# Sums of squares of q and k in fp32, a softplus series with one instruction a step, and four row casts on ScalarE, in a hybrid attention and DeltaNet block

## The chip, the cores and the metric

The kernel runs on one core of one Trainium2 chip. The metric is device time in microseconds (us) of one execution. Engines are named as in the profile: PE (TensorE matmul), PEld (its weight loads), DVE (VectorE), ACT (ScalarE), POOL (GpSimd) and SP (SyncE, which here only issues DMAs). Each engine works through its own queue strictly in the order written, and waits on semaphores for the others.

## The reference, cut to what matters

One layer of a streaming encoder: 16 meta tokens and 512 tokens of width 1024 go through RMSNorm, then through two parallel branches (forgetting attention, and a gated delta rule over chunks of 64), then a ConvFFN. The change touches the front end of the gated delta rule and nothing else:

```python
def l2_norm(x):
    return x * lax.rsqrt(jnp.sum(x * x, axis=-1, keepdims=True) + RMS_EPS)

gdn_qkv = jax.nn.silu(causal_dwconv(gdn_qkv, gdn_conv_w))       # q, k, v: 8 heads of 64
log_f = jax.nn.log_sigmoid(fox_f + fgt_bias)
beta  = jax.nn.sigmoid(gdn_b)
g     = -jnp.exp(gdn_a_log) * jax.nn.softplus(gdn_a + gdn_dt_bias)
q = l2_norm(q) * (dk ** -0.5);  k = l2_norm(k)
gc = jnp.cumsum(g, axis=-1)                                      # within each chunk
decay = jnp.exp(jnp.where(tril, gc[..., :, None] - gc[..., None, :], NEG_INF))
lmat = jnp.where(strict, jnp.einsum('bhncd,bhnsd->bhncs', kb, k) * decay, 0.0)
```

So there are sums of squares over the 64 channels of each head, for q and for k, at all 528 tokens. All three small gates come from a softplus of 3 x 8 values per token. From the logarithms of these sums and from `gc` the kernel makes rows of 8 heads by 576 padded tokens, whose differences are the exponents of `decay`.

## The kernel before, in words

**Products.** Activations lie with channels on the 128 partitions and the 528 tokens along the free axis. A weight tile of 128 output channels is loaded as fp32 and split in two: `hi` is a rounded fp32r copy, made on ACT (L131), and `lo = raw - hi`, made on DVE, or on POOL for the input tiles 5 to 8 (L132, `POOL_LO`). `product` then issues three fp32r matmuls for each 128 x 128 block (L139 to L141): hi by hi, hi by lo, lo by hi. An input projection is 48 such matmuls, in two halves of 264 tokens.

**Order.** The input projections run in a written order (`PLAN` and the list `order`): first the small gates (tile 0), then k (tiles 1 to 4), q (5 to 8), v (9 to 12), then output gates and attention projections, which fill PE while the delta rule goes on. The framework's scheduler turns the program into one queue per engine. It uses its own estimate of when each operand is ready, so an edit in one place can move instructions far behind it in all queues.

**The part that changes.** `gdn_tile(kind, pair, ss)` handles one tile of two heads, eight times: four of k (`kind` 0) and then four of q (`kind` 1). DVE scales the projection into `y` (L626). ACT starts a four-tap causal convolution in `cv` (L631), DVE adds three taps (L633), ACT takes a tanh (L636), and DVE multiplies into `kq` (L641, L642). Then come the squares. ACT squares `kq` twice, once into the fp32r tile `sqh` and once into the fp32 tile `sq` (L647, L648). POOL makes `sql = sq - sqh` (L649), and PE sums both over the 64 channels of each head, with a 128 x 8 matrix of zeros and ones (`selR`, fp32r) as the stationary operand, into two PSUM banks (L653, L654). `sqh` and `sql` live in single buffers (tags LS and X). After four tiles ACT takes the logarithms of the sums (L684 to L686). The logarithm and the tanh need different ACT tables, so an ACT_TABLE_LOAD stands wherever the one follows the other.

**Softplus.** The gate projection is transposed to 120 columns on 128 partitions. The logarithm is a series in s2 on DVE: a multiply (L578) and an add (L579) for each of seven coefficients, then L580 and L581. Its result `sp` is transposed back on PE (`ps_m` L591, `ps_r` L593) and scaled on DVE (L594 to L596). Three groups use one `ps_m` tile, so each group's transpose waits for the DVE reads of the group before.

**Rows.** L692 to L702 make the 8 x 576 rows. Four of these instructions are plain casts to fp32r on DVE (L698 twice, L700, L701). Their results go to POOL, which builds the operands of the chunk products (L725, L728), on which PE's `ps_d` and `ps_e` (L735, L739) rest.

**Later.** Nine chunks are prepared and scanned, attention runs in four pairs of heads (scores `ps_s`, values `ps_fo`, the transposed v `ps_fv`), and the rest is branch products (`bg`, `bf`), the output projection and the ConvFFN.

Of the kernel before, what the change touches and what calls it, by code (L numbers as in the profile page):

```python
# [12 lines left out]
F32 = mybir.dt.float32  # L13
F32R = mybir.dt.float32r
I32 = mybir.dt.int32
AF = mybir.ActivationFunctionType
ALU = mybir.AluOpType
# [4 lines left out]
P = 128  # L22
D = 1024
KT = D // P
T = 528
NM = 16
# [7 lines left out]
TP = NCH * C  # L34
EPS = 1e-6
GATES = list(range(8, 16)) + list(range(8))
TMPB = {'y': 2, 'cv': 2, 'th': 1, 'sq': 1}
SZB = 2
SOLVEP = 300
BF_A = 3  # L40
# [3 lines left out]
INORDER = ()  # L44
W0K = 2
CC_AT = 1
SS_DVE = ()
N_WARM = 8
LAG = 0
X_AHEAD = 1  # L50
# [31 lines left out]
C_HM, C_PM, C_SG, C_SEL, C_M0, C_M1, C_HM2, C_R1, C_R2, C_AB = 0, 2, 6, 7, 39, 151, 279, 281, 409, 473  # L82
# [4 lines left out]
def hybrid_block(ctx: ExitStack, tc: tile.TileContext, xT, w_in, w_bg, w_bf, w_out, w_up, w_down,  # L87
                 par, consts, out, dbg=None):
    nc = tc.nc
    act, dve, pool, pe = nc.scalar, nc.vector, nc.gpsimd, nc.tensor  # L90
# [13 lines left out]
    cst = keep.tile([P, C_N], F32, name="cst")  # L104
# [131 lines left out]
    with tc.tile_pool(name="inp", bufs=1) as inp:  # L236
# [19 lines left out]
        for k in range(KT):  # L256
# [14 lines left out]
            sq = acc if k in (0, SQ_POOL[0]) else inp.tile([P, T], F32, tag="sq", bufs=3, name="sq")  # L271
# [223 lines left out]
    with ExitStack() as gctx:  # L495
        gp = gctx.enter_context(tc.tile_pool(name="gp", bufs=1))

        subp = proj_ctx.enter_context(tc.tile_pool(name="sp", bufs=1, side="right"))

        ep_ctx = ExitStack()  # L500
        ep = ep_ctx.enter_context(tc.tile_pool(name="ep", bufs=1, side="right"))
# [4 lines left out]
        def main(ap):  # L506
            return ap.rearrange("p (n c) -> p n c", c=C)
# [3 lines left out]
        pool.memset(hmE.bitcast(F32), 0.0)  # L511
        dve.tensor_copy(hmE[0:40].rearrange("p (a b) -> p a b", b=C),
                        cst[0:40, C_HM:C_HM + 2].unsqueeze(2).broadcast_to([40, 2, C]))
        selR = ep.tile([P, 32], F32R, name="selR")
        pool.tensor_copy(selR, cst[:, C_SEL:C_SEL + 32])
        nA = gp.tile([8, 1], F32, name="nA")
        act.activation(nA, prm[0:8, PG_AL:PG_AL + 1], AF.Exp)
        dve.tensor_scalar(nA, nA, -1.0, None, op0=ALU.mult)
# [5 lines left out]
        R1, R2, KB, AB = [], [], [], ep.tile([104, 2, TP], F32R, name="AB")  # L524
# [48 lines left out]
        dve.reciprocal(s2, s2)  # L573
        dve.tensor_tensor(se, se, s2, op=ALU.mult)
        dve.tensor_tensor(s2, se, se, op=ALU.mult)
        dve.tensor_scalar(sr, s2, 1.0 / 17, 1.0 / 15, op0=ALU.mult, op1=ALU.add)
        for m in (13, 11, 9, 7, 5, 3, 1):
            dve.tensor_tensor(sr, sr, s2, op=ALU.mult)  # L578
            dve.tensor_scalar(sr, sr, 1.0 / m, None, op0=ALU.add)  # L579
        dve.scalar_tensor_tensor(sr, se, 2.0, sr, op0=ALU.mult, op1=ALU.mult)  # L580
        dve.scalar_tensor_tensor(sp.rearrange("p a b -> p (a b)"), sxf, 0.0, sr, op0=ALU.max, op1=ALU.add)  # L581


# [22 lines left out]
        for j in range(5):  # L606
            w = min(P, T - j * P)
# [11 lines left out]
        CUT = NM + 256  # L619

        def gdn_tile(kind, pair, ss=None):
# [19 lines left out]
            dve.scalar_tensor_tensor(d0, th[:, 0:NM], 1.0, a[:, 0:NM], op0=ALU.add, op1=ALU.mult)  # L641
            dve.scalar_tensor_tensor(d1, main(th[:, NM:]), 1.0, main(a[:, NM:]), op0=ALU.add, op1=ALU.mult)  # L642
            sq = tmp("sq", f"sq{idx}")

            sqh, sql = (subp.tile([P, 1024], F32R, tag=t, name=n)[:, 0:T] for t, n in (("LS", f"sqh{idx}"), ("X", f"sql{idx}")))
            for t in (sqh, sq):
                act.activation(t[:, 0:NM], d0, AF.Square)  # L647
                act.activation(main(t[:, NM:T]), d1, AF.Square)  # L648
            (dve if kind * 4 + pair in SS_DVE else pool).tensor_tensor(sql, sq, sqh.bitcast(F32), op=ALU.subtract)  # L649
            sel = selR[:, pair * 8:pair * 8 + 8]  # L650
            for i, t in enumerate((sqh, sql)):
                first, last = pair == 0 and i == 0, pair == 3 and i == 1
                pe.matmul(ss[0][0:8, 0:CUT], sel, t[:, 0:CUT], start=first, stop=last)  # L653
                pe.matmul(ss[1][0:8, 0:256], sel, t[:, CUT:], start=first, stop=last)  # L654

        def v_tile(p):

# [37 lines left out]
        dve.scalar_tensor_tensor(br, lnk, -0.5, gc, op0=ALU.mult, op1=ALU.subtract)  # L695
        dve.tensor_tensor(main(kl), main(br), main(gc)[:, :, C - 1:C].broadcast_to([8, NCH, C]), op=ALU.add)
        for w in range(2):
            dve.tensor_copy(AB[0:8, w], ar[w])  # L698
            dve.tensor_tensor(AB[32:40, w], ar[w], AB[0:8, w].bitcast(F32), op=ALU.subtract)
        dve.tensor_copy(bh, br)  # L700
        dve.tensor_copy(AB[64:72, 0], bh.bitcast(F32))  # L701
        dve.tensor_tensor(AB[96:104, 0], br, bh.bitcast(F32), op=ALU.subtract)  # L702

        tokf = gp.tile([C, NCH, 2, 8], F32, name="tokf")
# [659 lines left out]
```

## Time and profile before

| what | value |
|---|---|
| three timed runs | 877.65, 878.01, 878.02 us (median 878.01) |
| the profiled execution | 877.7 us; its span is 875.8 us, so 1.9 us lie outside the span |
| PE busy | 839.6 us of the span (96%) |
| DVE, ACT, POOL busy | 585.5 us (67%), 392.6 us (45%), 140.5 us (16%) |
| PE clock granted | full nearly everywhere, mean 0.991 |

The page's digits by slice say that PE is at 9 tenths or more nearly everywhere, with dips in the first three slices, and DVE is at 9 tenths in most of the first six. The table of stages and the timeline by engine say more than the page does, because the change lies between 36 and 110 us. In a timeline row the first number is the start in us from the beginning of the span and the second is the duration in us. Then come engine, line, operation, tiles and shape. A bracket at the end holds the idle time before the instruction and what released it. Rows of matmuls overlap, since a matmul's duration runs from its issue to its last write: what one costs PE is the distance between two starts.

### The profile page before, as it was taken

Reading aid. Unit: us, or ns where it says so; the run is one execution under the profiler, and the core shown is the slowest. Engines: PE = TensorE matmul, PEld = TensorE weight load, DVE = VectorE, ACT = ScalarE, POOL = GpSimd, SP = SyncE. Lnnn points to the kernel's source line nnn. Section 1 sums busy time; section 2 is a strip of 40 time slices with the busy share of each in tenths; the row PEclk is TensorE's granted clock in tenths of the full one; section 3 lists DMA queues with packets and bytes.
Section 4 is the critical chain, followed back from the end, with each engine's and each line's share of the span. In section 5 each row is a group of like instructions: output and inputs, shape, how many; then the busy total and the mean of one; then the engine's idle time right before and its main releaser. Section 6 shows DMA issues by size and latency. Waiting matters only on the chain. (4 is left out here: it accounts for less than half of the span.)

```text
span 875.8 us, 17084 instructions
## 1 busy us (share of the span) xinstructions
PE 839.6 (96%) x7088; PEld 801.0 (91%) x7088; DVE 585.5 (67%) x1066; ACT 392.6 (45%) x611; POOL 140.5 (16%) x167
## 2 busy tenths in 40 slices
PE   7978999999999999899999999999999999999995
PEld 7977999999999999788999999999999999888884
DVE  7999998697266678787654676677766677232324
ACT  6655554523433485855354454434444344332321
POOL 4353575100000201100522100000000000010113
PEclk9999999999999999989999999999999999999997
DMA  7312233627432341335623223333223332333322
GB/s 229 107 49 73 74 97 99 149 93 176 127 116 74 92 140 61 98 103 150 218 98 97 89 83 95 97 97 95 80 92 98 97 96 77 99 91 107 91 67 96
DMA packets 52240, 91.27 MB, mean 104 GB/s; under 512 B 24438, under 2 KB 27646, under 8 KB 52164
## 3 DMA queue, kind: packets, MB, share of 16 engines
q1 hardware_dynamic: 51060, 89.14, 33.9%
q8 instruction: 55, 0.90, 0.5%
q10 hardware_dynamic: 1104, 1.05, 0.4%
q14 instruction: 21, 0.17, 0.1%
HBM read 80.01 MB, written 10.16 MB: 103 GB/s over the span
## 5 line engine op out<-in xcount | busy, mean ns | idle before, releaser
L140 PE MATMUL ps_in<-xl,hi_in 128*128 128x264 f32 (+2 forms) x720 | 197.8, 285 | 2.5 <-DVE xl L264 2.5
L139 PE MATMUL ps_in<-xh,hi_in 128*128 128x264 f32 (+2 forms) x720 | 197.4, 287 | 1.7 <-ACT hi_in L131 1.2
L140 PE MATMUL ps_up<-ul,hi_up 128*128 128x256 f32 (+1 forms) x704 | 198.7, 282 | 0.0
L141 PE MATMUL ps_in<-xh,lo_in 128*128 128x264 f32 (+2 forms) x720 | 196.7, 286 | 1.9 <-DVE lo_in L132 1.9
L141 PE MATMUL ps_up<-uh,lo_up 128*128 128x256 f32 (+1 forms) x704 | 198.4, 282 | 0.0
L139 PE MATMUL ps_up<-uh,hi_up 128*128 128x256 f32 (+1 forms) x704 | 198.0, 282 | 0.0
L140 PEld LDWEIGHTS ps_in<-xl,hi_in 128*128 128x128 f32 x720 | 132.8, 188 | 4.0 <-DVE xl L264 3.1
L139 PEld LDWEIGHTS ps_in<-xh,hi_in 128*128 128x128 f32 x720 | 132.0, 188 | 4.5 <-ACT hi_in L131 1.9
L141 PEld LDWEIGHTS ps_in<-xh,lo_in 128*128 128x128 f32 x720 | 132.0, 188 | 3.8 <-DVE lo_in L132 2.6
L139 PEld LDWEIGHTS ps_up<-uh,hi_up 128*128 128x128 f32 x704 | 133.0, 189 | 0.0
L141 PEld LDWEIGHTS ps_up<-uh,lo_up 128*128 128x128 f32 x704 | 132.8, 189 | 0.0
L140 PEld LDWEIGHTS ps_up<-ul,hi_up 128*128 128x128 f32 x704 | 132.7, 188 | 0.0
L1197 DVE TENSOR_TENSOR u<-ps_up,rstd 128x258 f32<-128x258 f32 x88 | 37.2, 425 | 56.6 <-PE ps_up L141 56.6
L139 PE MATMUL ps_dn<-fh,hi_dn 128*128 128x512 f32 (+1 forms) x198 | 73.5, 371 | 0.0
L140 PE MATMUL ps_dn<-fl,hi_dn 128*128 128x512 f32 (+1 forms) x198 | 73.0, 369 | 0.0
L141 PE MATMUL ps_dn<-fh,lo_dn 128*128 128x512 f32 (+1 forms) x198 | 73.0, 369 | 0.0
L132 DVE TENSOR_TENSOR lo_dn<-raw_dn,hi_dn 128x1024 fp32r<-128x1024 f32 (+1 forms) x25 | 29.0, 1160 | 61.2 <-ACT hi_dn L131 61.2
L131 ACT ACTIVATE hi_in<-raw_in 128x1024 fp32r<-128x1024 f32 x43 | 45.0, 1054 | 51.3 <-PE ps_in L140 33.4
L1232 POOL TENSOR_TENSOR acc<-acc,sq 128x512 f32<-128x512 f32 (+1 forms) x7 | 11.2, 1607 | 353.1 <-ACT sq L1230 353.1
L131 ACT ACTIVATE hi_up<-raw_up 128x1024 fp32r<-128x1024 f32 x44 | 46.7, 1061 | 37.8 <-PE ps_up L140 28.3
L132 DVE TENSOR_TENSOR lo_up<-raw_up,hi_up 128x1024 fp32r<-128x1024 f32 x44 | 53.9, 1225 | 14.3 <-ACT hi_up L131 14.3
L131 ACT ACTIVATE hi_dn<-raw_dn 128x1024 fp32r<-128x1024 f32 (+1 forms) x25 | 24.8, 993 | 74.9 <-PE ps_dn L140 70.0
(339 smaller groups left out, 1655.8 us busy)
## 6 DMA issues: line engine op xcount, KB each, us to landing
raw_up<-w_up SPq DMA_DIRECT2D x44, 512.0 KB, 3.5
raw_in<-w_in SPq DMA_DIRECT2D x43, 512.0 KB, 4.0
raw_dn<-w_down SPq DMA_DIRECT2D x17, 512.0 KB, 3.5
gd<-g SPq DMA_DIRECT2D x16, 257.0 KB, 4.2
gt<-gd SPq DMA_DIRECT2D x16, 257.0 KB, 2.7
raw_o<-w_out SPq DMA_DIRECT2D x8, 512.0 KB, 3.5
raw_dn<-w_down SPq DMA_DIRECT2D x8, 384.0 KB, 3.1
xr<-xT SPq DMA_DIRECT2D x8, 264.0 KB, 4.4
```

What stands on the lines that cost most here:

```text
L131: act.activation(hi[:, a:a + step], raw[:, a:a + step], AF.Copy)
L132: (eng or dve).tensor_tensor(lo[:, a:a + step], raw[:, a:a + step], hi[:, a:a + step].bitcast(F32), op=ALU.subtract)
L139: pe.matmul(ps, wh[:, ws], xh[:, k0 + i, a:b], start=first and i == 0, stop=False)
L140: pe.matmul(ps, wh[:, ws], xl[:, k0 + i, a:b], start=False, stop=False)
L141: pe.matmul(ps, wl[:, ws], xh[:, k0 + i, a:b], start=False, stop=last and i == k - 1)
L1197: dve.tensor_tensor(y[:, a:b], ps[:, :b - a], rstd2[:, a:b], op=ALU.mult)
L1232: pool.tensor_tensor(acc[:, a:b], acc[:, a:b], sq, op=ALU.add)
```

## The change

Three edits, in one function of the program:

- `gdn_tile` squares once, into an fp32 tile `sq` with two buffers (`TMPB`). `sqh`, `sql`, the POOL subtraction and `selR` are gone. The sums are one matmul per PSUM bank and tile, with fp32 operands on both sides, in place of two in fp32r.
- The softplus series is arranged so that each of its seven steps is one instruction, (sr + 1/m) * s2. One extra instruction doubles `se`, and the last product adds the leading 1.
- The four casts of the rows are activations on ACT; the second of the casts of `br` reads the fp32 row itself instead of the rounded one.

```diff
-TMPB = {'y': 2, 'cv': 2, 'th': 1, 'sq': 1}
+TMPB = {'y': 2, 'cv': 2, 'th': 1, 'sq': 2}
...
-        selR = ep.tile([P, 32], F32R, name="selR")
-        pool.tensor_copy(selR, cst[:, C_SEL:C_SEL + 32])
...
-        dve.tensor_scalar(sr, s2, 1.0 / 17, 1.0 / 15, op0=ALU.mult, op1=ALU.add)
-        for m in (13, 11, 9, 7, 5, 3, 1):
-            dve.tensor_tensor(sr, sr, s2, op=ALU.mult)
-            dve.tensor_scalar(sr, sr, 1.0 / m, None, op0=ALU.add)
-        dve.scalar_tensor_tensor(sr, se, 2.0, sr, op0=ALU.mult, op1=ALU.mult)
+        dve.tensor_scalar(sr, s2, 1.0 / 17, None, op0=ALU.mult)
+        for m in (15, 13, 11, 9, 7, 5, 3):
+            dve.scalar_tensor_tensor(sr, sr, 1.0 / m, s2, op0=ALU.add, op1=ALU.mult)
+        dve.tensor_scalar(s2, se, 2.0, None, op0=ALU.mult)
+        dve.scalar_tensor_tensor(sr, sr, 1.0, s2, op0=ALU.add, op1=ALU.mult)
...
             sq = tmp("sq", f"sq{idx}")
-
-            sqh, sql = (subp.tile([P, 1024], F32R, tag=t, name=n)[:, 0:T] for t, n in (("LS", f"sqh{idx}"), ("X", f"sql{idx}")))
-            for t in (sqh, sq):
-                act.activation(t[:, 0:NM], d0, AF.Square)
-                act.activation(main(t[:, NM:T]), d1, AF.Square)
-            (dve if kind * 4 + pair in SS_DVE else pool).tensor_tensor(sql, sq, sqh.bitcast(F32), op=ALU.subtract)
-            sel = selR[:, pair * 8:pair * 8 + 8]
-            for i, t in enumerate((sqh, sql)):
-                first, last = pair == 0 and i == 0, pair == 3 and i == 1
-                pe.matmul(ss[0][0:8, 0:CUT], sel, t[:, 0:CUT], start=first, stop=last)
-                pe.matmul(ss[1][0:8, 0:256], sel, t[:, CUT:], start=first, stop=last)
+            act.activation(sq[:, 0:NM], d0, AF.Square)
+            act.activation(main(sq[:, NM:T]), d1, AF.Square)
+            sel = cst[:, C_SEL + pair * 8:C_SEL + pair * 8 + 8]
+            pe.matmul(ss[0][0:8, 0:CUT], sel, sq[:, 0:CUT], start=pair == 0, stop=pair == 3)
+            pe.matmul(ss[1][0:8, 0:256], sel, sq[:, CUT:], start=pair == 0, stop=pair == 3)
...
-            dve.tensor_copy(AB[0:8, w], ar[w])
+            act.activation(AB[0:8, w], ar[w], AF.Copy)
             dve.tensor_tensor(AB[32:40, w], ar[w], AB[0:8, w].bitcast(F32), op=ALU.subtract)
-        dve.tensor_copy(bh, br)
-        dve.tensor_copy(AB[64:72, 0], bh.bitcast(F32))
+        act.activation(bh, br, AF.Copy)
+        act.activation(AB[64:72, 0], br, AF.Copy)
```

The change is nine lines shorter, so the line numbers of its later part are 9 lower (the logarithms at L684 to L686 become L675 to L677). The scheduler gives every queue a new order from the first projections up to the branch products `bf`; behind these, PE's order is that of the kernel before. Three places matter below.

**DVE, around the third tile of k.** `cv2` and `cv3` are the convolutions of tiles 2 and 3 of k, `y3` and `y4` evacuate projections, `kq` takes the product with the tanh, and `ogT` rows are softplus steps. Before:

```order
L578 TENSOR_TENSOR ogT_108<-ogT_108 128x120
L626 TENSOR_TENSOR y3_619<-ps_in4_627,rstdh_115 128x264
L633 SCALAR_TENSOR_TENSOR cv2_598<-y2_539,prm_73,cv2_598 128x527
L579 TENSOR_SCALAR ogT_108<-ogT_108 128x120
L633 SCALAR_TENSOR_TENSOR cv2_598<-y2_539,prm_73,cv2_598 128x526
L578 TENSOR_TENSOR ogT_108<-ogT_108 128x120
L633 SCALAR_TENSOR_TENSOR cv2_598<-y2_539,prm_73,cv2_598 128x525
```

The change:

```order
L572 TENSOR_TENSOR ogT_108<-ogT_108 128x120
L630 SCALAR_TENSOR_TENSOR cv2_576<-y2_517,prm_73,cv2_576 128x527
L573 TENSOR_SCALAR ogT_108<-ogT_108 128x120
L623 TENSOR_TENSOR y3_590<-ps_in4_598,rstdh_115 128x264
L630 SCALAR_TENSOR_TENSOR cv2_576<-y2_517,prm_73,cv2_576 128x526
L575 SCALAR_TENSOR_TENSOR ogT_108<-ogT_108 128x120
L630 SCALAR_TENSOR_TENSOR cv2_576<-y2_517,prm_73,cv2_576 128x525
```

The first tap of tile 2 has moved ahead of the evacuation of `y3`, and the softplus begins its steps later in the queue, with one instruction for each.

**ACT, at the logarithms of k's sums.** `ps_ss` are the sums, `th` the tanhs, `sq` and `sqh` the squares. Before:

```order
L684 ACT_TABLE_LOAD
L684 ACTIVATE LA_442<-ps_ss_489,epsb_76 8x64
L685 ACTIVATE LA_442<-ps_ss_489,epsb_76 8x256
L686 ACTIVATE LA_442<-ps_ss_490,epsb_76 8x256
L636 ACT_TABLE_LOAD
L636 ACTIVATE th5_848<-cv5_843 128x528
```

The change:

```order
L675 ACT_TABLE_LOAD
L675 ACTIVATE LA_434<-ps_ss_481,epsb_76 8x64
L676 ACTIVATE LA_434<-ps_ss_481,epsb_76 8x256
L633 ACT_TABLE_LOAD
L633 ACTIVATE th4_732<-cv4_727 128x528
L677 ACT_TABLE_LOAD
L677 ACTIVATE LA_434<-ps_ss_482,epsb_76 8x256
L641 ACTIVATE sq4_736<-kq_478 128x16
L642 ACTIVATE sq4_736<-kq_478 128x512
```

The tanh of the first q tile (`th4`) now stands between the logarithms; a table is loaded for it, and another for the last logarithm, which stands ahead of the squares of that tile.

**PE, where the last attention projection (`in44`, the last v) ends.** `ps_fv` transposes v, in two halves, and `ps_fo` are attention values, with `ph0` and `pl0` the two parts of the probabilities. Before:

```order
L141 MATMUL ps_in44_4935<-xh_112,lo_in44_4872 128x264
L431 MATMUL ps_fv_4986<-ident_74,vf3_4933 128x128 x2
L488 MATMUL ps_fo_4652<-ph0_3918,vh0_1991 128x512
L431 MATMUL ps_fv_4986<-ident_74,vf3_4933 128x128 x2
L432 MATMUL ps_fw_4987<-ident_74,vf3_4933 16x128
L450 MATMUL ps_s_5034<-qh1_3905,ks1_3904 128x512
```

The change:

```order
L140 MATMUL ps_in44_4871<-xh_112,lo_in44_4808 128x264
L487 MATMUL ps_fo_4588<-ph0_3854,vh0_1927 128x512
L430 MATMUL ps_fv_4922<-ident_74,vf3_4869 128x128 x2
L487 MATMUL ps_fo_4588<-pl0_3855,vh0_1927 128x512
L487 MATMUL ps_fo_4588<-ph0_3854,vl0_1928 128x512
L487 MATMUL ps_fo_4588<-ph0_3854,vh0_1927 128x400
```

The values of the pair, which need `pl0` from DVE, have moved ahead of the second half of the transposes of v, which needs `vf3` from DVE.

More of the change, by code (lines that the diff above doesn't have):

```diff
@@ L46 @@
 CC_AT = 1
-SS_DVE = ()
 N_WARM = 8
```

## The prediction

> **What bounds the kernel now.** I read the busy times first, then a table of stages, then the waits of PE in the stage that changes. The first line of the page:
>
> ```profile
> PE 839.6 (96%) x7088; PEld 801.0 (91%) x7088; DVE 585.5 (67%) x1066; ACT 392.6 (45%) x611; POOL 140.5 (16%) x167
> ```
>
> PE has almost no room, so time is PE's work plus its idle time. The table of stages (stretch, its length, then busy us of each engine, the granted clock, the DMA share, GB/s):
>
> ```profile
> 38.00:99.00 61.00, 52.34 (x433) 49.08 (x432) 59.68 (x101) 33.24 (x65) 27.41 (x18) 1.00 0.22 70
> 99.00:150.00 51.00, 48.48 (x389) 46.55 (x388) 44.26 (x79) 27.49 (x46) 33.62 (x54) 1.00 0.32 92
> 150.00:350.00 200.00, 198.46 (x2266) 189.62 (x2265) 137.37 (x333) 88.94 (x154) 15.51 (x34) 1.00 0.41 113
> 370.00:375.00 5.00, 2.21 (x8) 1.63 (x9) 4.42 (x8) 4.08 (x10) 0.00 (x0) 0.62 0.37 114
> 375.00:380.00 5.00, 5.00 (x29) 4.82 (x29) 5.00 (x11) 1.25 (x3) 0.00 (x0) 0.70 0.71 229
> ```
>
> In 38 to 99, where the edits lie, PE is idle for 8.7 us while DVE is busy for 59.68 of 61 us: DVE, not PE, sets the pace there. In 99 to 150 PE idles 2.5 us, then hardly at all until 370. PE's own timeline names the waits of the first stage:
>
> ```profile
> 51.57 0.29 PE L653 MATMUL ps_ss<-sqh,selR 128*8 128x272 f32 x1 [2.14 <-ACT sqh L648]
> 57.89 0.29 PE L653 MATMUL ps_ss<-sqh,selR 128*8 128x272 f32 x1 [2.13 <-ACT sqh L648]
> 61.96 0.27 PE L591 MATMUL ps_m<-ident,ogT 128*8 128x128 f32 x1 [0.58 <-DVE ogT L581]
> 67.84 0.27 PE L591 MATMUL ps_m<-ident,ogT 128*8 128x128 f32 x1 [2.20 <-DVE LA L595]
> 72.21 0.27 PE L591 MATMUL ps_m<-ident,ogT 128*8 128x128 f32 x1 [0.75 <-DVE LA L595]
> 76.46 0.29 PE L653 MATMUL ps_ss<-sql,selR 128*8 128x272 f32 x1 [0.85 <-POOL sql L649]
> ```
>
> They add up to 8.65 us. Every one is an instruction of the code that changes, late because a DVE or POOL result is late. Each costs a little more than its bracket: a bracket starts at the modelled end of the matmul before, 0.28 after its start, though the next could have started at 0.12 (rows below). That is 0.16 each, so the six cost 9.6 us.
>
> **The sums on PE.** Before, a tile takes four fp32r matmuls. PE's timeline at the first:
>
> ```profile
> 41.16 0.29 PE L653 MATMUL ps_ss<-sqh,selR 128*8 128x272 f32 x1
> 41.28 0.28 PE L654 MATMUL ps_ss<-sqh,selR 128*8 128x256 f32 x1
> 41.40 0.28 PE L139 MATMUL ps_in<-xh,hi_in 128*128 128x264 f32 x1
> ```
>
> From start to start 0.12 us each, so 0.48 us a tile. An fp32 matmul of the same columns stands at the end of the kernel, in the chain that ended last (start, time on the chain, what):
>
> ```profile
> 854.63 0.70 PE ps_n L1257 x2
> 861.85 0.43 PE ps_n L1254 x2
> 862.28 0.12 PE ps_dn L139
> ```
>
> There one fp32 matmul of 256 columns (recorded as two) takes 0.43 us between fp32r matmuls of 0.12. With 272 columns it is 0.46, so a tile takes 0.89 us and eight tiles cost 8 x (0.89 - 0.48) = **+3.3 us** of PE work. The bounds: nothing, if the 8-column operand lets them run like the fp32r ones at equal count, which leaves -1.9 us (sixteen fewer at 0.12); and 0.70 apiece as in the first row, which gives +7.4. I take the row inside a stream of matmuls, since that is where they will stand. Nothing hides this: PE is the engine that ends last.
>
> **What DVE gets back.** Groups by line, for POOL in 36 to 110 and for DVE in 38 to 99 (count, busy us and mean ns), and then single rows of the timelines:
>
> ```profile
> L649 POOL TENSOR_TENSOR sql<-sq,sqh 128x528 fp32r<-128x528 f32 x8 | 15.0, 1874 | 26.8 <-ACT sq L648 21.2 <-issue 3.0 <-PE ps_in L140 2.6
> L132 POOL TENSOR_TENSOR lo_in<-raw_in,hi_in 128x1024 fp32r<-128x1024 f32 x4 | 10.1, 2524 | 9.4 <-ACT hi_in L131 9.4
> L633 DVE SCALAR_TENSOR_TENSOR cv<-y,prm,cv 128x525 f32<-128x525 f32 (+2 forms) x24 | 23.5, 979 | 0.7 <-ACT cv L631 0.6
> L578 DVE TENSOR_TENSOR ogT<-ogT 128x120 f32<-128x120 f32 x7 | 4.9, 704 | 0.0
> L579 DVE TENSOR_SCALAR ogT<-ogT 128x120 f32<-128x120 f32 x7 | 3.6, 508 | 0.0
> ```
>
> ```profile
> 45.67 1.48 DVE L633 SCALAR_TENSOR_TENSOR cv<-y,prm,cv 128x527 f32<-128x527 f32 x1
> 47.88 0.27 DVE L578 TENSOR_TENSOR ogT<-ogT 128x120 f32<-128x120 f32 x1
> 48.07 0.75 DVE L633 SCALAR_TENSOR_TENSOR cv<-y,prm,cv 128x525 f32<-128x525 f32 x1
> 48.75 0.21 DVE L579 TENSOR_SCALAR ogT<-ogT 128x120 f32<-128x120 f32 x1
> 53.71 2.29 DVE L579 TENSOR_SCALAR ogT<-ogT 128x120 f32<-128x120 f32 x1
> 53.50 2.42 POOL L132 TENSOR_TENSOR lo_in<-raw_in,hi_in 128x1024 fp32r<-128x1024 f32 x1
> 102.88 0.44 DVE L698 CAST AB<-LA 8x576 fp32r<-8x576 f32 x1
> ```
>
> The same L579 takes 0.21 us alone and 2.29 when POOL started a subtraction just before it; it ends when POOL ends. The three groups are above their undisturbed lengths by 24 x 0.23, 7 x 0.43 and 7 x 0.30, together 10.6 us. POOL's two groups are busy 15.0 and 10.1 us, so the subtractions that the change removes should be 60% of that, 6.4 us. Besides, seven of fourteen softplus steps go (at 0.13 from start to start, 0.9 us; L579 at 48.75 is followed at 48.88) and four casts at 0.44 (1.8 us). DVE sheds some 9 of its 59.7 us, and stops being the pace. The casts go to ACT, which is busy 33.24 of 61; they cost nothing unless the last one is late for POOL's chunk operands, and then about their 0.44.
>
> The page "SBUF — State Buffer" of the Trainium skill (Who interferes with whom) says more: a DVE instruction with two SBUF inputs that meets a GpSimd instruction that reads SBUF blocks until that one has ended. The 2.29 beside the 2.42 agrees in kind. By that rule up to all 15.0 us of the subtractions could come back to DVE, which is the first rival below and not my sum.
>
> **What PE then still waits for.** I walk the new queues with these durations; PE takes 0.12 a matmul.
>
> *The squares of k's third tile (51.57).* They are ready earlier by 0.73 (the tap at 45.67 loses its 1.48 - 0.75), by 0.64 (on ACT two squares no longer stand ahead of the tanh before; rows below, less 0.1 of overlap), by 0.75 (this tap now stands ahead of the blocked step) and 0.3 (two steps fewer): at about 49.1. PE gets there at 41.16 + 2 x 0.89 + 43 x 0.12 = 48.1. Wait 1.0.
>
> *`ps_m`, on softplus.* From there PE needs 0.89, 25 matmuls and half a pair, to 53.4. DVE still has two taps, two evacuations, the `kq` product and seven small steps, some 4.5 us, and one block of 2.4 by the `lo` of tile 7, which stays on POOL. Wait 1.8.
>
> *The squares of q's first tile.* Here ACT's order costs. Its rows:
>
> ```profile
> 39.89 0.62 ACT L648 ACTIVATE sq<-kq 128x512 f32<-128x512 f32 x1
> 61.23 0.64 ACT L636 ACTIVATE th<-cv 128x528 f32<-128x528 f32 x1 [2.87 <-DVE cv L633]
> 64.73 1.28 ACT L684 ACT_TABLE_LOAD   x1
> 66.23 0.45 ACT L685 ACTIVATE LA<-ps_ss,epsb 8x256 f32<-8x256 f32 x1
> ```
>
> After DVE's last tap (2.4 us behind softplus) come a load, the tanh, a load, a logarithm and the squares: 1.28 + 0.64 + 1.28 + 0.45 + 0.72 = 4.4 us. PE has 32 matmuls, two groups of transposes and half a pair to do, 5.2 us. Wait 6.8 - 5.2 = 1.6. The second tile of q needs one more load, and with the same steps I find 0.7. Beyond it PE finds everything ready.
>
> Sum 5.1, with four times 0.16, 5.7 us in place of 9.6: **-3.9 us**. Bounds: all of it gone (-9.6), or waits as large as before plus the two extra loads (+0.8, the fourth rival).
>
> **Behind the stage.** The 2.5 us of 99 to 150 belong to DVE and POOL results as well; a less loaded DVE should save some, and I take **-0.7** (bounds -2.5 and 0). At 370 the new order matters:
>
> ```profile
> 373.16 0.69 PE L431 MATMUL ps_fv<-ident,vf 128*128 128x128 f32 x2 [2.79 <-DVE vf L422]
> 370.48 0.69 DVE L1038 TENSOR_TENSOR ofT<-ofT,den 128x512 f32<-128x512 f32 x1 [2.33 <-DMA den<-rd]
> 376.37 1.81 DVE L470 TENSOR_TENSOR s<-s,mb 128x512 f32<-128x512 f32 x5
> 373.02 1.67 DVE L482 TENSOR_TENSOR pl<-s,ph 128x1184 fp32r<-128x1184 f32 x3
> ```
>
> DVE's queue waits for a DMA, and behind it stand what PE needs. Before, this was `vf`, 2.7 us after the DMA. In the new order PE needs `pl` first, behind 0.69 + 1.81 + 1.67 = 4.2 us. But what PE did in between is then still to do, or has been done: I take **+0.5** (bounds -2.8, the whole wait, and +2).
>
> **Sum.** +3.3 - 3.9 - 0.7 + 0.5 = -0.8 on the profiled 877.7 (span 875.8 and 1.9 around it): 876.9. The median of the runs is 0.3 above the profiled one, so the forecast is **877.2 us**: no change that can be told, since about 0.2% (1.8 us) is what a measurement here can tell from none.
>
> **Rivals.**
>
> *POOL was nearly the whole cause.* DVE gets the 15 us back, and PE keeps only the wait behind the remaining `lo` (1.8 + 0.16): -7.6, and the 2.5 behind goes too. 877.7 + 3.3 - 7.6 - 2.5 + 0.5 = 871.4, or 871.7 as a median. For it speaks that DVE is 98% busy in the stage; against it that ACT's table loads sit on the path whatever DVE does. Half of this already reads as faster. Chance 0.26.
>
> *The slow clock goes.* At 370 to 380 the granted clock is 0.62 and 0.70, behind the wait of 2.79. In 5 us each that is about 7 us at half speed, of which PE worked in some 4.8 (from 373.16), a loss of 2.4. A different order may shorten this wait: 877.2 - 2.4 - 0.5 = 874.3. The page "TensorE: Matmul & The Clock Gate" of the Trainium skill (What you observe, and what follows it) says that a free-running window of about 3.4 us decides; the idle time here is near that, so by it the slow stretch could come or go with a small shift. The three runs within 0.4 us say that it does not do so by chance. Chance 0.14.
>
> *The fox stage waits longer.* `pl` for PE is late by all of the +2 above, and the slow clock lasts as long again as half of what it costs now (1.2): 877.2 + 1.5 + 1.2 = 879.9. For it speaks the 4.2 against 2.7; against it that PE gets other work done later. Chance 0.09.
>
> *Slower, by ACT's table loads.* The tanh of q's first tile is behind taps that the `lo` of tile 8 blocks once more (2.4), and the squares of two tiles stand behind it and its loads. The waits are 1.0, 1.8, 1.6 + 2.4 and 0.7 + 2.4, with 0.64 in all 10.5, +0.9 in place of -3.9: 877.2 + 4.8 = 882.0. It decides for slower once the waits of this stage add to more than 8.3 (then -1.3 + 3.3 - 0.7 + 0.5 is over 1.8). Chance 0.17. That the fp32 sums cost 0.70 each adds 4.1 to any case; I count it within these.
>
> **How the numbers follow.** My forecast has 0.34. Faster: 0.26 + 0.14 = 0.40. Slower: 0.17 + 0.09 = 0.26. Same: 0.34. The range goes from the first rival to the slower one, 871.5 to 882; the forecast's own is 875.5 to 879. It leaves out a tail on each side, that of a dear fp32 matmul and that of waits wholly gone.
>
> **What would show it.** Right: fp32 `ps_ss` in two records each, 0.43 to 0.46 per matmul from start to start; undisturbed L633 taps of 0.75 except beside the `lo` of tiles 6 to 8; PE idle in 38 to 99 near 5 us; an ACT_TABLE_LOAD on each side of `th4`, and a wait at the sums behind it. Wrong: PE idle in that stage below 2 or above 8 us, taps as long as before with POOL quiet, or a clock at 370 to 380 that is full.

## The result: slower by 1.6%, outside the range

The changed kernel takes 891.51 us (median of four runs, 888.97 to 893.83), the kernel before 877.83 us beside it (four runs). The ratio is 1.0157, 95% interval 1.0119 to 1.0196. Forecast were 877.2 us, with a range of 871.5 to 882. Runs of one kernel differ by a few us, and the longer ones have a lower granted clock (here 0.981 in two runs near 894, 0.985 in two near 889), so medians are compared.

The profiled execution is the fastest of the four (888.97 us). Its span is 887.2 us, in place of 875.8, so it shows 11.4 of the 13.7 us. Its first line, then the table of stages with the columns of the prediction's:

```profile
PE 849.0 (96%) x7088; PEld 804.9 (91%) x7088; DVE 578.4 (65%) x1056; ACT 393.3 (44%) x601; POOL 126.9 (14%) x158
```

```profile
38.00:99.00 61.00, 57.10 (x433) 48.82 (x431) 54.72 (x98) 36.12 (x61) 17.73 (x16) 1.00 0.21 64
99.00:150.00 51.00, 46.78 (x351) 45.04 (x350) 42.68 (x79) 25.25 (x42) 30.96 (x50) 0.93 0.27 76
150.00:350.00 200.00, 192.12 (x2192) 182.74 (x2191) 124.20 (x297) 80.72 (x136) 11.19 (x28) 0.98 0.42 117
...
375.00:380.00 5.00, 5.00 (x44) 4.98 (x43) 3.39 (x10) 2.53 (x5) 1.51 (x3) 1.00 0.22 75
380.00:440.00 60.00, 55.59 (x446) 52.69 (x445) 46.06 (x109) 32.59 (x60) 7.96 (x9) 0.94 0.47 143
```

In the stage that the prediction worked on, PE idles 3.9 us in place of 8.7: the early gain is there. The loss is behind it. The stages from 99 to 350 had a full clock and little idle time; now they have 0.93 and 0.98 and idle 4.2 and 7.9 us. The slow stretch at 370 to 380 is gone, and another stands at 386.

PE's order is the same in both kernels from the first `bf` products on, but for a few of these that change places, and in the midst of them PE waits for `gt` in both. Up to that wait the two can be set against each other (stretch, length, PE busy; before and after):

```profile
99.00:430.56 331.56, 320.31 (x3231) 305.37 (x3229) 241.21 (x549) 163.47 (x285) 62.09 (x99) 0.99 0.41 116
```

```profile
99.00:443.38 344.38, 326.14 (x3233) 311.04 (x3231) 239.05 (x543) 161.15 (x279) 58.75 (x91) 0.97 0.39 112
```

The changed kernel arrives 12.8 us later, which is more than the whole difference of the spans. PE's idle time grew by 7.0 us behind 99 (11.25 to 18.24) and shrank by 4.8 in 38 to 99. Four stretches run at half the clock, 20.5 us in all, in place of one of 6.8. PE's timeline behind 99 names the long waits, and a table by stretch shows the clock behind each:

```profile
115.65 0.50 PE L730 MATMUL ps_e<-r,hmE 104*128 104x512 f32 x1 [2.06 <-POOL r L716]
...
132.54 0.50 PE L730 MATMUL ps_e<-r,hmE 104*128 104x512 f32 x1 [1.71 <-POOL r L716]
...
171.62 0.58 PE L138 MATMUL ps_in<-xh,hi_in 128*128 128x256 f32 x1 [3.05 <-DVE g L322]
...
388.43 0.79 PE L487 MATMUL ps_fo<-pl,vh 128*128 128x512 f32 x1 [3.19 <-DVE pl L481]
```

```profile
116.23:119.64 3.41, 3.41 (x19) 3.41 (x18) 3.33 (x7) 0.97 (x2) 3.10 (x5) 0.50 0.43 118
133.29:136.71 3.42, 3.42 (x17) 3.32 (x17) 2.18 (x4) 1.57 (x4) 2.99 (x4) 0.50 0.98 283
170.84:177.67 6.83, 5.61 (x24) 5.31 (x25) 4.93 (x12) 1.34 (x2) 0.00 (x0) 0.50 0.48 132
385.88:392.71 6.83, 4.28 (x16) 4.04 (x17) 6.83 (x15) 5.20 (x10) 0.00 (x0) 0.50 0.36 110
```

PE is busy for 16.7 us of these and half of that is lost, 8.4 us; in the kernel before it was busy for 4.86 of the one stretch and lost 2.4. That is another 5.9.

Why these waits? POOL's rows, then DVE's:

```profile
111.11 0.57 POOL L764 TENSOR_TENSOR sub<-L,X 8x15 f32<-8x15 f32 x1 [7.11 <-DMA L<-ld]
...
114.33 0.26 POOL L764 TENSOR_TENSOR sub<-L,X 8x48 f32<-8x48 f32 x1
114.56 1.03 POOL L716 TENSOR_TENSOR r<-AB,cst 40x512 fp32r<-40x512 f32 x1
...
129.85 0.95 POOL L759 MEMSET X<- 128x1024 f32 x1 [1.42 <-DMA x0d<-X]
...
130.94 1.55 POOL L716 TENSOR_TENSOR r<-AB,cst 40x512 fp32r<-40x512 f32 x1
```

```profile
169.12 0.19 DVE L764 TENSOR_TENSOR sub<-LS,X 128x31 f32<-128x31 f32 x1 [6.16 <-DMA LS<-ld]
...
170.96 0.27 DVE L766 TENSOR_TENSOR X<-X,sub 128x112 f32<-128x112 f32 x1
171.15 0.75 DVE L322 TENSOR_TENSOR g<-ps_in,rstdh 128x256 f32<-128x256 f32 x2
```

Two solvers belong to the delta rule (the `sub` and `X` rows are their steps): a small one for the meta chunk on POOL, and one for all blocks on DVE. Each begins with data that come back by DMA. On POOL the operand `r` of a chunk stands behind seven steps of the meta solver, and those behind a DMA wait of 7.11 us. The next `r` stands behind all of that solver and a memory fill that waits for its output's DMA. On DVE the evacuations (`g`) of the second halves of two gate projections stand behind eight solver steps, and those behind a DMA wait of 6.16 us. `r`, and the PSUM banks that the evacuations free, are what PE needs next.

On DVE this order is new. In the kernel before, the last of these evacuations started at 159.3, sixteen instructions ahead of the solver's first step. On POOL it isn't: there `r` stood behind eight steps of the meta solver too, and the later one behind the fill, but PE waited 0.60 us for the first and came 2.8 us after the second was made. The kernel before:

```profile
123.14 0.50 PE L739 MATMUL ps_e<-r,hmE 104*128 104x512 f32 x1 [0.60 <-POOL r L725]
```

```profile
175.10 0.19 DVE L773 TENSOR_TENSOR sub<-LS,X 128x31 f32<-128x31 f32 x1 [3.05 <-DMA LS<-ld]
```

So on POOL what is new is how soon PE comes to `r`. One theory was formed, **A**: it is the order of the queues that costs the time, by waits behind these DMAs and by the slow clock behind the waits. Against it stood **B**, that one edit costs the time by itself (fp32 sums, or the hop to ACT), and **C**, ACT's table loads.

### The profile page after: what moved, and what is told of

Same layout as the page of the kernel before. It is cut to its first block, busy times and chain, and to the rows that moved or that the text cites. A ratio compares the mean times of both kernels' runs of the same rounds, so it can differ in the third digit from the quotient of the medians.

```text
span 887.2 us, 17038 instructions
## 1 busy us (share of the span) xinstructions
PE 849.0 (96%) x7088; PEld 804.9 (91%) x7088; DVE 578.4 (65%) x1056; ACT 393.3 (44%) x601; POOL 126.9 (14%) x158
## 4 chain that ended last, share of the span: by engine, by line
PE 76%; DVE 11%; DMA 5%; ACT 3%; POOL 2%; issue 2%; SPq 0%; DVEq 0%; ACTq 0%; POOLq 0%
PE ps_up L139 10%; PE ps_up L138 9%; PE ps_up L140 9%; PE ps_in L138 5%; PE ps_in L140 5%; PE ps_in L139 5%; PE ps_dn L140 5%; PE ps_dn L139 5%; PE ps_dn L138 5%; DVE cv L630 3%; PE ps L830 2%; PE ps_fo L487 2%; PE ps_o L139 2%; PE ps_o L140 2%; PE ps_o L138 2%
## 5 line engine op out<-in xcount | busy, mean ns | idle before, releaser
L138 PE MATMUL ps_in<-xh,hi_in 128*128 128x264 f32 (+2 forms) x720 | 200.9, 291 | 5.1 <-DVE g L322 3.0
L138 PEld LDWEIGHTS ps_in<-xh,hi_in 128*128 128x128 f32 x720 | 134.4, 191 | 9.2 <-DVE g L322 3.3
L139 PEld LDWEIGHTS ps_in<-xl,hi_in 128*128 128x128 f32 x720 | 134.9, 191 | 3.8 <-DVE xl L263 2.3
```

The lines of the kernel that those rows point to most:

```text
L138: pe.matmul(ps, wh[:, ws], xh[:, k0 + i, a:b], start=first and i == 0, stop=False)
L139: pe.matmul(ps, wh[:, ws], xl[:, k0 + i, a:b], start=False, stop=False)
```

## Experiments

The time of the kernel before is that measured beside each run. "Ratio" is to that kernel, with the 95% interval.

**One edit at a time.** The first three are the hunks of the change, each alone: the squares and sums; the softplus steps; the four casts. The fourth has none of them:

```diff
-N_WARM = 8
+N_WARM = 9
```

> The kernel before with the first edit alone: the sums of squares from unsplit squares in fp32. Theory A (the order of the queues): the sums cost PE 3.3 us, the first stage gives back about 4, and all else comes from new waits between 100 and 190 us and at 370 to 390 us and from the slow clock behind them. This edit reorders DVE's queue most of the three, so the time is likely well above 878: 883 to 892, with PE waits of over 1 us behind 100 us whose releaser is a DVE or POOL result queued behind a step that waits for a DMA. Theory B (the fp32 sums themselves are dear): 888 to 892, and the excess lies at the sums in 38 to 99 us. Theory C (ACT's table loads are dear): 878 to 883, the excess in 38 to 99 us, with waits at the sums of q.

> The kernel before with the second edit alone: seven fewer steps in the softplus series. Its direct effect is at most 0.9 us of DVE time, so by theories B and C 877 to 878. By theory A the new order can cost or gain several us: anywhere in 873 to 886, and whatever differs by over 2 us lies in PE waits behind 100 us, not in 38 to 99.

> The kernel before with the third edit alone: four row casts on ScalarE. DVE sheds 1.8 us, ACT gets about 2 us. Theories A, B: the queues change least of the three, so 877 to 880. If the hop from DVE to ACT and back is what delays the chunk operands, 880 to 885, with waits at ps_d or ps_e between 99 and 125 us that the kernel before doesn't have.

> The kernel before with one more matmul at the very start (nine warm-up matmuls in place of eight, their result is used by nothing): a change with next to no work (about 0.4 us at most, while PE waits for its first data) that still gives the queues of DVE and ACT a new order from there to the branch products. Theory A: the time moves by 2 us or more, up or down, with the difference in waits behind 100 us. Theories B and C: 878, as before, since nothing that they name has changed.

| kernel | median us | before us | ratio |
|---|---|---|---|
| fp32 sums alone | 876.11 | 877.65 | 0.9997 (0.9976 to 1.0018) |
| softplus alone | 876.65 | 877.65 | 0.9988 (0.9978 to 0.9999) |
| casts alone | 877.27 | 877.65 | 0.9991 (0.9979 to 1.0003) |
| ninth warm-up matmul | 891.48 | 877.65 | 1.0149 (1.0129 to 1.0168) |

No edit costs anything alone, so B and C fall as causes of the 13.7 us. Theory A's guess of 883 or more for the sums alone was wrong too: their order misses the gate wait. And one idle matmul more costs as much as the whole change. Two of PE's long waits with it:

```profile
141.51 0.50 PE L739 MATMUL ps_e<-r,hmE 104*128 104x512 f32 x1 [2.94 <-POOL r L725]
...
420.19 0.79 PE L488 MATMUL ps_fo<-ph,vh 128*128 128x512 f32 x1 [3.45 <-ACT ph L481]
```

The first is POOL's place again; the second is in the attention, which this edit reaches only through the order.

**The order mended, the edits kept.** The helper `behind(eng)` queues what follows on that engine behind the last instruction written for it so far; it sets the order only. First the meta solver on POOL, then the block solver on DVE, then both, and POOL's once more on the ninth warm-up matmul:

```diff
-PLAN = "p0 m v0 p1 v1 v2 p2 p3 p4 ...
+PLAN = "p0 v0 p1 v1 v2 p2 p3 m p4 ...
...
-            solve(pool, L0, X0, 16, ...)
+            with behind(pool):
+                solve(pool, L0, X0, 16, ...)
```

```diff
-PLAN = "... p8 f t0 F F s0 f f f q0 ...
+PLAN = "... p8 f F F s0 f f f t0 q0 ...
...
-            with tc.high_priority(offset=SOLVEP):
+            with tc.high_priority(offset=SOLVEP), behind(dve):
                 solve(dve, LS, X, 32, ...)
```

> The changed kernel, with the small solver of the meta chunk traced three chunks later and queued on POOL behind the fourth chunk's operands. The queues of DVE and ACT are those of the changed kernel, instruction for instruction; only POOL's order and four DMA issues change. Theory A: the waits of 2.06 and 1.71 us for POOL's r at ps_e (115.65 and 132.54) go, and with them the two slow-clock stretches of 3.4 us that follow them: -3.8 and up to -3.4, so 884 to 888 in place of 891.5, with the waits at 171.62 and 388.43 still there. Theory B (one of the edits costs the time by itself, by PE's fp32 sums or ACT's casts): 891, since all three edits are still in it.

> The changed kernel, with the block solver queued on DVE behind the evacuations of the second gate tile, as it stands in the kernel before. POOL's queue is that of the changed kernel. Theory A: PE's wait of 3.05 us for the gate evacuation at 171.62 and the slow clock behind it (6.8 us, worth up to 3.4) go: 885 to 889 in place of 891.5; DVE's queue behind this place also changes, so the waits at 325 to 390 may change by 2 us either way. Theory B: 891.

> The changed kernel with both: the meta solver behind the fourth chunk's operands on POOL, and the block solver behind the gate evacuations on DVE. Theory A: both gains, 878 to 883. What is left above the kernel before would be the 3.3 us of the fp32 sums less the early stage's gain, and the waits at 325 to 390. Theory B: 891.

> The kernel before with nine warm-up matmuls, and with the meta solver on POOL behind the fourth chunk's operands; the queues of DVE, ACT and SP are those of the kernel with nine warm-up matmuls alone, which took 891.5. Theory A: its wait of 2.94 us for POOL's r at 141.51 and the slow clock behind it go (-2.9 and up to -1.7): 886 to 889, with the attention waits at 352 to 421 still there. If these waits matter less than they seem, 890 to 892.

| kernel | median us | before us | ratio |
|---|---|---|---|
| change, POOL's order | 888.45 | 877.39 | 1.0125 (1.0107 to 1.0143) |
| change, DVE's order | 884.57 | 877.39 | 1.0080 (1.0064 to 1.0096) |
| change, both | 879.75 | 877.39 | 1.0028 (1.0013 to 1.0042) |
| ninth warm-up, POOL's order | 892.85 | 877.39 | 1.0176 (1.0158 to 1.0194) |

With all three edits in place, 11.3 of the 13.7 us above the kernel before go by order alone, and 2.4 are left. POOL's order by itself takes 2.6, DVE's 6.5. The first came out 0.5 us above its forecast, the second 0.4 below. The waits answer to it. With POOL's order alone the wait of 1.71 has become 0.85 and that of 2.06 is gone, while the gate's stays. With both, the gate's is gone too, and a smaller one for `lo_in` stands near its place. First the rows with POOL's order alone, then those with both:

```profile
128.96 0.49 PE L730 MATMUL ps_e<-r,hmE 104*128 104x512 f32 x1 [0.85 <-POOL r L716]
...
167.77 0.58 PE L138 MATMUL ps_in<-xh,hi_in 128*128 128x256 f32 x1 [3.64 <-DVE g L322]
```

```profile
128.13 0.50 PE L730 MATMUL ps_e<-r,hmE 104*128 104x512 f32 x1 [0.89 <-POOL r L716]
...
165.68 0.38 PE L140 MATMUL ps_in<-xh,lo_in 128*128 128x258 f32 x1 [1.49 <-DVE lo_in L131]
```

With DVE's order the wait of 3.19 for `pl` at 388 went as well (one of 2.50 for `vf` stands at 383.90 in that kernel); DVE's queue behind the solver is new there. Part of the 6.5 is that.

On the ninth warm-up matmul the forecast of 886 to 889 missed. Its wait of 2.94 went down to 1.03 as meant, but PE then waited 3.73 us for `pl` in the attention, with 6.8 us of slow clock, where it had waited 1.83 with none. First the row without POOL's order, then those with it:

```profile
386.70 0.50 PE L488 MATMUL ps_fo<-pl,vh 128*128 128x512 f32 x1 [1.83 <-DVE pl L482]
```

```profile
141.04 0.50 PE L739 MATMUL ps_e<-r,hmE 104*128 104x512 f32 x1 [1.03 <-POOL r L725]
...
388.78 0.79 PE L488 MATMUL ps_fo<-pl,vh 128*128 128x512 f32 x1 [3.73 <-DVE pl L482]
```

So theory A doesn't say that mending one place gains what that place costs. Which order in that kernel makes the attention wait was not taken apart and stays open.

**Is it a threshold?** In the orders of the kernels one can count how far the last evacuation of the first two gate tiles stands from the first step of the block solver in DVE's queue, in instructions. By the table below, each edit brings the solver nearer to that evacuation or past it. Two pairs of edits fall on either side, and the third kernel makes the changed order in the kernel before. It marks the solver's eighth step and queues the second evacuation of these gate tiles behind it:

```diff
+                if eng is dve and j == 3:
+                    fox.mark = next(i for i in reversed(nc.cur_bb.bb.instructions) if i.engine == dve.engine)
...
         def evac(ps, a, b):
-            dve.tensor_tensor(gt[:, a - OFF:b - OFF], ps, rstdh[:, a:b], op=ALU.mult)
+            with tc.issue_after(fox.mark) if i in (8, 9) and a > OFF else nullcontext():
+                dve.tensor_tensor(gt[:, a - OFF:b - OFF], ps, rstdh[:, a:b], op=ALU.mult)
```

> The kernel before with two edits, the fp32 sums and the casts, each of which alone left the time where it was (876.1 and 877.3 against 877.7). Theory A (a threshold in the order): with both, the last gate evacuation stands eight instructions behind the block solver's first step on DVE (with the squares alone three ahead of it, in the kernel before sixteen ahead, with all three edits nine behind), so PE waits 2 us or more for it, with a slow clock behind: 880 to 888. Theory B (what an edit costs is its own): the sum of the two, 875 to 878.

> The kernel before with two edits, the softplus steps and the casts. Theory A: here the last gate evacuation still stands seven instructions ahead of the block solver's first step, so the wait for it doesn't come: 875 to 879 unless one of the later attention waits turns out differently (then up to 883). Theory B: the sum of the two, 876 to 877. The run tells whether any two edits cost the time or only those that carry the solver past the gates.

> The kernel before, none of the three edits, with one constraint of order: the evacuations of the second halves of the first two gate tiles are queued on DVE behind the eighth step of the block solver, as in the changed kernel. Theory A: PE waits 3 us or more for the gate evacuation near 175 and the clock goes slow behind it; 880 to 888 (the solver's data land later than in the changed kernel, so the wait may be longer than the 3.05 there). The queues behind this place are new as well, so 2 us of it may be of other waits. If that place doesn't matter: 877 to 879.

| kernel | last gate evacuation, from the solver's first step | median us | ratio |
|---|---|---|---|
| before | 16 ahead | 877.79 | |
| casts | 14 ahead | 877.27 | 0.9991 |
| softplus | 13 ahead | 876.65 | 0.9988 |
| softplus, casts | 7 ahead | 875.19 | 0.9969 (0.9946 to 0.9991) |
| sums | 3 ahead | 876.11 | 0.9997 |
| sums, casts | 8 behind | 883.39 | 1.0075 (1.0053 to 1.0097) |
| all three | 9 behind | 891.51 | 1.0157 |
| before, gates put behind | 11 behind | 885.97 | 1.0103 (1.0066 to 1.0140) |

Two harmless edits together cost 5.6 us, and the kernel before, with no edit, costs 8.2 more when it gets this order. So the step lies between 3 ahead and 8 behind; no kernel stands between these. The PE waits of these two kernels:

```profile
163.58 0.58 PE L138 MATMUL ps_in<-xh,hi_in 128*128 128x256 f32 x1 [3.40 <-DVE g L322]
```

```profile
175.06 0.38 PE L139 MATMUL ps_in<-xh,hi_in 128*128 128x256 f32 x1 [2.92 <-DVE x L336]
```

The first kernel also waits 3.19 us for `pl` at 381.31, with 3.4 us of slow clock, as the changed kernel does at 388; so its 5.6 us aren't the gate's alone. In the second the evacuation named is that of the next tile, which stands behind the gates'. There the wait and its slow clock (3.4 us long) make some 4.6 of the 8.2; the rest is a wait of 2.82 at `ph` near 419 and slow clock behind it, in the new order behind this place. So the place is shown to cost, and the constraint also moves other waits.

**A version that beats both.** The fp32 sums alone leave one long wait for POOL's `r` (3.10 us at 134.91), which mends with the diff above (`m` behind `p3`):

> The fp32 sums alone (876.1), with the meta solver on POOL behind the fourth chunk's operands. The queues of DVE and ACT are, instruction for instruction, those of the sums alone. There PE waited 3.10 us for POOL's r at 134.91. Theory A: that wait goes: 871.5 to 874, faster than both kernels. If the gain is given back by a later wait for a DMA, as it was with nine warm-up matmuls, 875 to 877.

It takes 873.15 us, ratio 0.9944 (0.9923 to 0.9964): 4.6 us below the kernel before, and 18 below the changed one. The wait before the mending and after:

```profile
134.91 0.49 PE L730 MATMUL ps_e<-r,hmE 104*128 104x512 f32 x1 [3.10 <-POOL r L716]
```

```profile
133.52 0.50 PE L730 MATMUL ps_e<-r,hmE 104*128 104x512 f32 x1 [1.51 <-POOL r L716]
```

**The price of the fp32 form, and what pins the stage.** Two kernels save other work ahead of this place. One is the kernel of 873.15 us with the rounded squares alone, and leaves out what the rounding cuts off. The other has the softplus steps and casts with POOL's order mended. The edit of the first:

```diff
-            sq = tmp("sq", f"sq{idx}")
-            sel = cst[:, C_SEL + pair * 8:C_SEL + pair * 8 + 8]
+            sq = tmp("sq", f"sq{idx}", F32R)
+            sel = selR[:, pair * 8:pair * 8 + 8]
```

> The kernel of the sums alone with the meta solver moved on POOL (873.15), but the squares are written as fp32r and summed in fp32r: the part of the sums that the rounding cuts off is left out. It tells the price of the fp32 form on PE. In the changed kernel's rows a pair of fp32 sums moves the matmuls behind it by about 1.19 us, where the prediction had 0.89; a pair in fp32r costs 0.24. If the 1.19 is real and on the path: eight times 0.95, up to 7.6 us less PE work, so 866 to 869. If 0.89 holds: 5.2 less, 868 to 870. If the early stage is then held by DVE and ACT, whose results the sums wait for, part of it turns into waits in 38 to 99 us: 870 to 873.

> The softplus steps and the casts (875.2) with the meta solver on POOL behind the fourth chunk's operands; the queues of DVE and ACT are those of the two edits alone. There PE waited 0.98 and 1.07 us for POOL's r at 119.79 and 136.21. Theory A: about 2 us less, 872.5 to 874, without the fp32 sums and so without their cost on PE; if a later wait takes it back, 875 to 876.

They take 874.40 (ratio 0.9966, 0.9953 to 0.9979) and 875.86 us (0.9989, 0.9976 to 1.0002), and neither gained what theory A meant. The first missed its whole forecast (866 to 873); the second missed 872.5 to 874 and fell into the range for a wait that takes the gain back. PE met a longer wait at the same time of the span:

```profile
134.41 0.79 PE L732 MATMUL ps_e<-r,hmE 104*128 104x512 f32 x1 [3.87 <-POOL r L718]
```

```profile
136.58 0.50 PE L739 MATMUL ps_e<-r,hmE 104*128 104x512 f32 x1 [2.69 <-POOL r L725]
```

The profiled execution of the second is its fastest, 871.5 us, so its trace doesn't hold all that the median does. So the fp32 form's price for the whole time stays unmeasured: PE saved the work and waited instead. That wait is near 134 to 137 us whatever PE saves, as if POOL's solver pinned the fifth chunk. The last three runs put the solver one chunk later (`p4 m` in place of `p3 m`), for the sums alone, for softplus and casts, and for all three edits with DVE's order:

> The fp32 sums alone, with the meta solver on POOL one chunk later still, behind the fifth chunk's operands; the operands of chunks 6 to 8 then stand between its steps, and the block solver's memory fill behind all of them. DVE's queue is that of the sums alone but for a few rows. With the solver behind the fourth chunk PE still waited 1.51 us for r at 133.52 (873.15). Theory A (POOL's solver pins the fifth chunk): that wait goes, 870 to 872.5. If the solver is now late for the first scan step, PE waits for it between 150 and 165 us: 873 to 877.

> The softplus steps and the casts, with the meta solver on POOL behind the fifth chunk's operands; DVE's queue unchanged. With the solver behind the fourth chunk, PE waited 2.69 us for POOL's r at 136.58 and nothing was gained (875.9 against 875.2). Theory A: this wait goes: 872 to 874. If the solver is then late for the first scan step: 875 to 878.

> All three edits, the block solver behind the gate evacuations, and the meta solver behind the fifth chunk's operands in place of the fourth's (879.75 with the fourth's, where PE waited 0.89 us at ps_e). Theory A: 0.9 us less at that place, 878 to 880. What then separates it from the sums alone (873) isn't POOL's r but what the softplus and cast edits did to DVE's order: 1.49 us of wait for lo_in at 165.68 with a slow clock behind, and the waits at 377.

| kernel | solver behind the 4th chunk's operands | behind the 5th's | ratio of the latter |
|---|---|---|---|
| sums | 873.15 | 872.32 | 0.9951 (0.9932 to 0.9969) |
| softplus, casts | 875.86 | 873.54 | 0.9955 (0.9938 to 0.9972) |
| all three, DVE's order mended | 879.75 | 875.71 | 0.9988 (0.9976 to 1.0001) |

In none of the three does PE wait over 0.6 us for `r` near 134 any more; in the first a smaller wait appears later:

```profile
150.52 0.50 PE L730 MATMUL ps_e<-r,hmE 104*128 104x512 f32 x1 [1.14 <-POOL r L716]
```

So POOL's solver did pin it. The third came out 2.3 us below its forecast of 878 to 880: its trace has neither the wait of 1.49 for `lo_in` nor the slow clock behind it. With both orders mended, the full change is no slower than the kernel before, in place of 13.7 us slower. Whether the sums gain over the kernel before by themselves, at one and the same order, these runs can't say: the kernel before with POOL's solver moved was not run.

## Why the prediction was wrong, point by point

**The step that failed is "Behind the stage".** It took -0.7 us for 99 to 150, since a less loaded DVE should save some, and +0.5 at 370, and the walk before it ended with "Beyond it PE finds everything ready". The new order was read at three places only, all of which carried a term of the early stage or of 370. Behind 99 us PE's idle time grew by 7.0 us and the half clock took 5.9 more. The order had been at hand: the solver's steps, which begin with a DMA, had passed the gate evacuations. Four kernels show that place: the change with DVE's order mended, alone and with POOL's; the sums with the casts; and the kernel before with the gates put behind.

**The fp32 sums** were of the right kind and too small. The changed kernel's rows at the first pair:

```profile
41.27 0.28 PE L140 MATMUL ps_in<-xh,lo_in 128*128 128x264 f32 x1
41.49 0.62 PE L644 MATMUL ps_ss<-sq,cst 128*8 128x272 f32 x2
41.95 0.59 PE L645 MATMUL ps_ss<-sq,cst 128*8 128x256 f32 x2
42.47 0.39 PE L138 MATMUL ps_in<-xh,hi_in 128*128 128x264 f32 x1
42.70 0.28 PE L139 MATMUL ps_in<-xl,hi_in 128*128 128x264 f32 x1
42.82 0.28 PE L140 MATMUL ps_in<-xh,lo_in 128*128 128x264 f32 x1
```

The two matmuls take 0.46 and 0.52, near the 0.46 and 0.43 forecast. But the matmul ahead takes 0.22 in place of 0.12, and that behind 0.23: together 0.21 more around the pair. From 41.27 to 42.82 are 1.55 us, three matmuls of 0.12 and 1.19 for the pair. So the term is 8 x (1.19 - 0.48) = +5.7, not +3.3. The other pairs that PE reaches without a wait have the same spacing, to 0.01. The row at the end of the kernel, from which the 0.43 came, doesn't carry over. The kernel before has it so:

```profile
861.56 0.28 PE L141 MATMUL ps_dn<-fh,lo_dn 128*128 128x256 f32 x1
861.68 0.59 PE L1254 MATMUL ps_n<-acc,ones 128*128 128x256 f32 x2
861.93 0.47 PE L139 MATMUL ps_dn<-fh,hi_dn 128*128 128x256 f32 x1
862.23 0.28 PE L140 MATMUL ps_dn<-fl,hi_dn 128*128 128x256 f32 x1
```

From 861.56 to 862.23 are 0.67 us, less two fp32r matmuls of 0.12 that is 0.43, with the neighbours' delay in it. A pair of sums costs 1.19 by the same count. Why it costs more than two single ones (0.89) no run shows.

**The waits in 38 to 99** went in the main as walked, and a little better: idle 8.7 to 3.9, near the 5 forecast. The waits named were 1.0, 1.8, 1.6 and 0.7; measured were none at k's third squares, 1.19 at `ps_m`, 1.03 and 0.77 at q's sums, and 0.90 at `ps_c`, which was not foreseen. That the missing wait (1.0) and the unforeseen one (0.9) nearly cancel is luck. The three waits that were foreseen:

```profile
55.13 0.27 PE L588 MATMUL ps_m<-ident,ogT 128*8 128x128 f32 x1 [1.19 <-DVE ogT L578]
...
62.04 0.62 PE L644 MATMUL ps_ss<-sq,cst 128*8 128x272 f32 x2 [1.03 <-ACT sq L642]
...
72.58 0.62 PE L644 MATMUL ps_ss<-sq,cst 128*8 128x272 f32 x2 [0.77 <-ACT sq L642]
```

ACT's load on each side of `th4` is there, with the wait behind that the walk gave it:

```profile
57.65 1.28 ACT L633 ACT_TABLE_LOAD   x1 [2.25 <-DVE cv L630]
...
59.60 1.28 ACT L677 ACT_TABLE_LOAD   x1
60.90 0.46 ACT L677 ACTIVATE LA<-ps_ss,epsb 8x256 f32<-8x256 f32 x1
```

**DVE's gain** was smaller, and came by other instructions than forecast: DVE is busy for 5.0 us less in 38 to 99 (54.72 in place of 59.68), not 9. The seven softplus steps take 1.9 us, where the fourteen took 8.5; with the one that doubles `se` six instructions are saved, not seven. Of the 23 taps, 19 take 0.74 to 0.77 us, as the prediction asked of undisturbed ones. But the other four take 1.20 to 2.87, each beside an instruction of POOL, so the mean is 967 ns, against 989 in the same window before:

```profile
L630 DVE SCALAR_TENSOR_TENSOR cv<-y,prm,cv 128x527 f32<-128x527 f32 (+2 forms) x23 | 22.2, 967 | 0.4 <-ACT cv L628 0.3
...
L575 DVE SCALAR_TENSOR_TENSOR ogT<-ogT 128x120 f32<-128x120 f32 x7 | 1.9, 273 | 0.1
```

POOL's four `lo` stayed, and blocks of DVE with them: the tap of 2.87 us, at 43.67, stands beside one of 2.74 us. The prediction took the 2.29 us of L579 as a case of an instruction with two SBUF inputs, but L579 reads one tile; the tap reads two.

**The rivals.** "POOL was nearly the whole cause" left PE 2 us of waits in the stage and nothing behind; it has 3.9 and 7.0 more behind. "Slower, by ACT's table loads" had the sign right and the cause wrong. "The fox stage waits longer" named a wait that came (3.19 for `pl`, with 6.8 us of slow clock), near 388 instead of 370; it was priced at 2.7 with its clock, as the only late wait. "The slow clock goes" saw the clock only as something that could leave the one place where it stood. It did leave (1.00 in 370 to 380, which the prediction named as a sign that it was wrong), and came at four others.

**The sum as it is.** Up to the `bf` wait: +5.7 sums, -4.8 early waits, +7.0 later waits, +5.9 slow clock, and -0.4 ahead of 38 us, together +13.4 against 12.8 measured. The forecast's terms for the same were +3.3, -3.9, -0.2 and nothing.

## What to carry to other kernels

Where a scheduler orders the queues, an edit's own work can be the smaller part of what it does to the time: one idle matmul cost 13.8 us here, and three edits that cost nothing each cost 13.7 together. In the new order, look first at each instruction that waits for a DMA and at what stands behind it on its engine: whatever PE needs must stand ahead of it, and can be pinned there. And price a wait of PE of 2 us or more with the slow clock behind it, at up to twice its length: 30 of 41 such waits in these profiles had it (below).

## What the runs showed of the hardware that was not expected

**The clock follows the waits.** In the 19 profiles 47 stretches of half clock lie between 38 and 440 us, each 3.4 or 6.8 us long. All but one begin during a PE wait of 0.5 us or more or within 3 us of its end. By the length of the wait, so many have such a stretch (one near two waits counts for both):

| PE's wait, us | waits | with a slow stretch |
|---|---|---|
| 0.5 to 1 | 136 | 16 |
| 1 to 1.5 | 53 | 7 |
| 1.5 to 2 | 22 | 10 |
| 2 to 2.5 | 22 | 13 |
| over 2.5 | 19 | 17 |

This is a count, not an experiment: no run filled a wait with work. The page "TensorE: Matmul & The Clock Gate" of the Trainium skill (HAM oscillation) gives the rule that PE must have no idle gap over about 3.4 us. The length of the stretches agrees with its window; the rule doesn't hold here as a safe bound, since waits of 1.7 and 2.06 us were followed by a slow stretch in the changed kernel, and over half of those between 2 and 2.5. The measurement decides.

**A pair of fp32 sums among fp32r matmuls** costs PE 1.19 us by the rows at 41.27 to 42.82 above, where the rounded sums, in fp32r, take 0.24. Of this, 0.21 stands at the matmul ahead of the pair and the one behind it. The single fp32 matmul at 861.68 costs 0.43 with all that it does to its neighbours, so this isn't a fixed price of going to fp32 and back; what makes the difference was not tested.
